# Hybrid pool/SSD block on one core: output projection's rows scaled, split and stored during the x, B, C columns, read back as finished 1 MB tiles

## The chip, the cores and the metric

The kernel runs on one core of a Trainium2 chip. The metric is the device time of one execution in microseconds (us); less is better. A profile comes from one profiled execution of its own.

## The reference, cut to what matters

```python
mod_lat = silu(c) @ w_ada + b_ada                  # g_l is its last third: the gate, one number per output column
hm   = rmsnorm(h) * (1 + scale) + shift            # 2048 latent and 256 context tokens, 1024 channels
p    = hm @ w_in                                   # pool input, pool gate, SSD gate, x/B/C (2048 columns), dt
xbc  = silu(depthwise_conv(p[..., x, B, C]))
y_s  = rmsnorm(bidirectional_scan(xbc, dt) * silu(z_ssd)) * ssd_norm_w
y_p  = pool_mixer(p[..., pool]) * pool_scale * silu(z_pool)
out  = rmsnorm(x + g_l * (concat([y_p, y_s]) @ w_out)) * final_norm_w
```

`pool_scale` and `ssd_norm_w` are one number per row of `w_out`, `g_l` is one per column. The kernel therefore multiplies them into `w_out` (2048 rows of 1024) once. It also splits each fp32 weight into a rounded part (hi) and the residual (lo), so that a product takes three matmuls: hi by hi, hi by lo, lo by hi.

## The kernel before, in words

Work runs in stages, each of them fed to TensorE as long rows of matmuls:

- **Start.** adaLN numbers, norms and modulated tokens `hm[0..3]` (each hi and lo) for 4 blocks of 512 tokens, and x/B/C columns 0 and 1.
- **The x, B, C columns**, `for ct in range(2, 16)` at L578 to L600: one tile of 128 columns of `w_in` at a time. `weights()` (L219) loads a raw 512 KB tile (`raw_weights`, L207), lets ScalarE round it to hi and GpSimd subtract for lo (`split_weights`, L212). TensorE then makes 24 matmuls over the context (columns below 12) and 24 for each of 4 token blocks. After each block ScalarE, VectorE and GpSimd do the convolution (L259), and `conv_store` (L246) writes the result to DRAM; for columns below 12 it is transposed and goes out through the SP queue in four DMAs a block. Column `ct` loads the weights of column `ct + 1` when it begins. Columns 5 to 8 also carry `late_pool_map` (L543), columns 10 to 13 two `gate_row` each (L563), which sum up the gate `gacc` from 512 KB loads.
- **The sweep** (upper token halves, L717 on): z, pool-gate and pool products, with the backward states between them. Here the gate is spread to all partitions (`gb`, two matmuls), and the lower 8 of the 16 row tiles of `w_out` are scaled (`rescale`, L723) and stored to `s_wo`.
- **The lower halves** (L760 on): the same products for the lower tokens, and box means on VectorE. `prepare(k)` (L856) loads a row tile of `w_out`, scales it if that is not done, and writes hi and lo into `wout0` or `wout1`.
- **The ramp** (`RAMP`, L1208): the first scan steps, an order written out by hand, with `prep_load`, `prep_scale`, `prep_hi`, `prep_lo` of tiles 5 to 8 among them; tiles 9 to 15 follow it. Then 64 steady steps of scan and output projection, by hand-written table too.

Outside the two hand-ordered parts a scheduler sets each engine's order from the program and its own estimate of time; on an engine or a DMA queue instructions then start in that order, and one that waits holds all behind it. Of the pools, `rawp` (`rpool`) has two 4 KB-per-partition buffers under the one tag `wraw`, taken in turn by every raw weight tile, gate row and row tile, and a new tile waits until the last reader of the tile two before it is done.

```python
rpool = rstack.enter_context(tc.tile_pool(name="rawp", bufs=2, side="right"))
wpool = wstack.enter_context(tc.tile_pool(name="wpool", bufs=2, side="right"))
```

Of the kernel before, what the change touches and what calls it, by code (L numbers as in the profile page):

```python
# [23 lines left out]
def hybrid_block(ctx, tc, d, out):  # L24
# [11 lines left out]
    def pp(name):  # L36
        return psum.tile([P, 512], F32, tag="pp", name=name)
# [24 lines left out]
    s_zp = dram("s_zp", [8, P, 1024])  # L62
    s_yp = dram("s_yp", [NCH, P, 8, P])
    s_af = dram("s_af", [P, 2, NC2, 16])
    s_gate = dram("s_gate", [P, 1024])
    s_wo = dram("s_wo", [8, P, 1024])
    s_rows = dram("s_rows", [2, NCH, 16, P])

    wstack = ExitStack()
# [256 lines left out]

    hc = dp.tile([P, 2, 8, 256], F32R, tag="hc", name="hc")
    dt_raw = const("dt_raw", [P, NC2, 32], pool=dp)
    wd = dp.tile([P, 8, P], F32R, tag="wd", name="wd")
    ctxt = Tokens(hc, 256, d["ctxT"], 1, "c", wpool.tile([P, 8, 256], F32, tag="w", name="xc"))  # L330
    ada = [slot(f"ada{a}", [P, 4, 2048], F32) for a in range(2)]
    cu = slot("cu", [P, 8192], F32)
# [230 lines left out]
    def gate_row(k):  # L563

        wg = rpool.tile([P, 1024], F32, tag="wraw", name=f"wg{k}")
        nc.sync.dma_start(wg, d["w_ada"][k * P:(k + 1) * P, 2048:3072])
        if k == 0:
            nc.vector.tensor_scalar(gacc, wg, scol[:, k, 0:1], None, op0=ALU.mult)
        else:
            nc.vector.scalar_tensor_tensor(gacc, wg, scol[:, k, 0:1], gacc, op0=ALU.mult, op1=ALU.add)  # L570
        if k == 7:
            brow = rpool.tile([1, 1024], F32, tag="wraw", name="brow")
            nc.sync.dma_start(brow, d["b_g"])
            nc.vector.tensor_tensor(gacc[0:1, :], gacc[0:1, :], brow, op=ALU.add)
# [5 lines left out]
    for ct in range(2, 16):  # L580
        next(tables, None)
        col = cols[ct]
        col.w = wx.pop(ct)
        if ct < 15:
            wx[ct + 1] = weights(d["w_xbc"][ct + 1], f"x{ct + 1}")
        if ct < 12:
            col.context()
            col.context_out()
        for b in range(4):
            col.block(b)  # L590
            col.block_out(b)
            col.conv()
            if ct > 12 and late:
                late.pop(0)()
        if 5 <= ct < 9:
            late_pool_map(2 + (ct - 5) // 2, (ct - 5) % 2)
        elif ct in (10, 11, 12, 13):
            for k in range(2):
                gate_row(2 * ct - 20 + k)
    gstack.close()  # L600
    cstack.close()
    dstack.close()
    tabs2 = ctx.enter_context(tc.tile_pool(name="tabs2", bufs=1))
    rowscale = const("rowscale", [P, 16], d["rowscale"], pool=tabs2)
    dskip = const("dskip", [P, 16], d["d_skip"].broadcast_to([P, 16]), pool=tabs2)
    allone = const("allone", [P, P], pool=tabs2)
    nc.vector.memset(allone, 1.0)
    mcol = const("mcol", [P, 1], pool=tabs2)
    nc.vector.memset(mcol, 1.0 / 256.0)
    hst = const("hst", [P, 4, 256], pool=tabs2)  # L610
# [102 lines left out]
    with tc.tile_pool(name="sweepp", bufs=2) as bp, tc.tile_pool(name="evp", bufs=3) as ep:  # L713
# [6 lines left out]
                count[0] -= 10  # L720
                next(sw, None)

        def rescale(raw, k):  # L723

            for j in range(2):
                js = raw[:, 512 * j:512 * j + 512]
                nc.vector.scalar_tensor_tensor(js, js, rowscale[:, k:k + 1], gb[j], op0=ALU.mult, op1=ALU.mult)

        upper = (2, 3)
        for j in range(8):  # L730
            w = weights(d["w_z"][j], f"z{j}_2")
            for b in upper:
                silus.append(z_block(ep, w, j, b, between if j else None))
                if j == 0 and b == 2:
                    next(sw)
            if j == 1:
                gacc = rpool.tile([P, 1024], F32, tag="wraw", name="gacc2")
                nc.sync.dma_start(gacc, s_gate)
                gb = [pp(f"gb{j}") for j in range(2)]
                for j in range(2):  # L740
                    mm(gb[j], allone, gacc[:, 512 * j:512 * j + 512], True, True)
            for k in {1: (), 7: (5, 6, 7)}.get(j, (j - 2,) if j else ()):
                raw = rpool.tile([P, 1024], F32, tag="wraw", name=f"wos{k}")
                nc.sync.dma_start(raw, d["w_out"][1024 + k * P:1152 + k * P, :])
                rescale(raw, 8 + k)
                nc.scalar.dma_start(s_wo[k], raw)
            for src, dst, fn in ((d["w_zp"][j], s_zp, AF.Silu), (s_wp[j], s_v, AF.Copy)):
                w = weights(src, f"p{j}_{fn}")
                for i, b in enumerate(upper):
                    t = ep.tile([P, 512], F32, tag="ev", name=f"e{j}_{b}_{fn}")  # L750
                    ps = pp(f"pp{j}_{b}_{fn}")
                    project(ps, w, hm[b], between)
                    nc.scalar.activation(t, ps, fn)
                    nc.scalar.dma_start(dst[j, :, 512 * i:512 * i + 512], t)
# [79 lines left out]
    bx = slot("bx", [P, 8192], F32)  # L834
    wout = [slot("wout0", [P, 4, 2, 1024], F32R)]

    raws = {}

    def prep_load(k):
        raws[k] = rpool.tile([P, 1024], F32, tag="wraw", name=f"wor{k}")  # L840
        nc.sync.dma_start(raws[k], s_wo[k - 8] if k >= 8 else d["w_out"][k * P:(k + 1) * P, :])

    def prep_scale(k):
        if k < 8:
            rescale(raws[k], k)

    def prep_hi(k):
        nc.scalar.copy(wout[k // 4][:, k % 4, 0, :], raws[k])

    def prep_lo(k, eng=None):  # L850
        wo = wout[k // 4][:, k % 4]
        eng = eng or (nc.gpsimd if k in (1,3,4,5,7,13,15) else nc.vector)
        eng.tensor_tensor(wo[:, 1, :], raws[k], wo[:, 0, :].bitcast(F32), op=ALU.subtract)  # L853

    def prepare(k):
        prep_load(k)  # L856
        prep_scale(k)
        prep_hi(k)
        prep_lo(k)

    with tc.tile_pool(name="boxp", bufs=1) as xp:
        for i, j in enumerate(order):
# [339 lines left out]
        wout.append(slot(f"wout{len(wout)}", [P, 4, 2, 1024], F32R))  # L1202

    kp = None
    other = {f.__name__: f for f in (prep_load, prep_scale, prep_hi, prep_lo, z, zg, logs, work, more)}

    RAMP = """
    0:load prep_load/5 1:load 0:scores 0:carried 0:shift 0:mask 0:exponents prep_scale/5 1:shift 0:steps_mix  # L1210
    prep_hi/5 logs 0:decay z/6/0 1:scores 1:carried zg/6/0 z/7/0 0:mix 0:from_states prep_load/6 
    0:mix2 1:mask 1:exponents 2:load prep_scale/6 1:steps_mix prep_hi/6 1:decay zg/7/0 2:scores 2:carried more
    1:from_states 1:mix 0:outputs z/6/1 prep_lo/5 prep_load/7 0:load_pool prep_lo/6
    0:gate 2:mask prep_scale/7 1:mix2 prep_load/8 1:load_pool 0:squares 2:shift
    2:steps_mix 0:square_sum 2:exponents 1:outputs 0:norm_mm z/7/1 more work prep_hi/8 prep_hi/7 zg/6/1 prep_lo/8
    0:state prep_lo/7 3:load 2:from_states 1:gate 0:pool_hi 1:squares zg/7/1 logs 0:norm1 
# [102 lines left out]
```

## Time and profile before

| | us |
|---|---|
| median of 3 runs (lowest, highest) | 1699.45 (1695.41, 1699.87) |
| the profiled execution's own time | 1695.88 |
| its span, first to last instruction | 1694.0 |
| busy in the span: TensorE (PE) | 1639.7 |
| VectorE (DVE) / ScalarE (ACT) / GpSimd (POOL) | 1222.8 / 766.9 / 596.5 |
| mean granted TensorE clock | 0.986 |

The busy time of PE is that of pipelined matmuls, whose ends are modelled. The stages can be told apart by the names that PE works on: `px` and `pc` are the x, B, C columns, `pz` and the pool products follow, `po` is the output projection. Times below count from the start of the span.

### The profile page before, as it was taken

To read this page: it belongs to the slowest core of one execution; us is meant where nothing else is said; L and a number is where in the kernel's file an instruction comes from. 1 tells how busy PE (TensorE), PEld (TensorE's weight loads), DVE (VectorE), ACT (ScalarE), POOL (GpSimd) and SP (SyncE) were. 2 spreads that over 40 slices of the span, in tenths; PEclk is the share of its full clock that TensorE was granted. 3 is DMA by queue.
4 is the path that set the end of the run, shared out by engine and by line. 5 is a ranking of instruction groups with operands and counts; after the bars stand their busy time and mean duration, and the time that the engine had idled before them with its cause. 6 is when DMAs were issued, how large, how long until landed. Compare 5 with 4: busy or idle time off the path is not lost. (4 is left out here: it accounts for less than half of the span.)

```text
span 1694.0 us, 25052 instructions
## 1 busy us (share of the span) xinstructions
PE 1639.7 (97%) x7798; PEld 1308.1 (77%) x7798; DVE 1222.8 (72%) x2516; ACT 766.9 (45%) x1857; POOL 596.5 (35%) x666
## 2 busy tenths in 40 slices
PE   8899999999998999999999989869999999999997
PEld 2788888888886788888887868757888888888886
DVE  1885655466685878776299998557788888888885
ACT  2763544434454444443212122455565556565663
POOL 1522111111124666665433334323333333333331
PEclk9999999999999999999999999989999999999999
DMA  9432344566554777778624355675667667666662
GB/s 375 177 118 69 77 101 96 135 166 149 155 126 144 241 252 235 247 246 275 212 84 151 113 186 185 187 225 172 193 194 208 194 198 206 193 210 191 197 192 83
DMA packets 313623, 303.11 MB, mean 179 GB/s; under 512 B 132753, under 2 KB 240145, under 8 KB 311186
## 3 DMA queue, kind: packets, MB, share of 16 engines
q1 hardware_dynamic: 239362, 233.60, 47.5%
q10 hardware_dynamic: 74128, 67.91, 12.0%
q8 instruction: 62, 1.02, 0.2%
q14 instruction: 71, 0.58, 0.1%
HBM read 207.81 MB, written 93.62 MB: 178 GB/s over the span
## 5 line engine op out<-in xcount | busy, mean ns | idle before, releaser
L52 PE MATMUL px<-hm,w_x 128*128 128x512 f32 x1536 | 365.6, 397 | 2.4 <-ACT hm L200 1.3
L52 PEld LDWEIGHTS px<-hm,w_x 128*128 128x128 f32 x1536 | 288.3, 188 | 71.9 <-DVE hm L203 1.5
L52 PE MATMUL po<-wout,yp 128*128 128x512 f32 x768 | 212.9, 413 | 0.0
L52 PE MATMUL po<-wout,ys 128*128 128x512 f32 x768 | 211.2, 411 | 0.0
L52 PE MATMUL pz<-hm,w_z 128*128 128x512 f32 x768 | 188.1, 398 | 1.1 <-POOL w_z L215 1.1
L265 DVE SCALAR_TENSOR_TENSOR cacc<-u,conv_w,cacc 128x512 f32<-128x512 f32 x168 | 135.5, 820 | 61.1 <-POOL u L315 42.1
L52 PEld LDWEIGHTS pz<-hm,w_z 128*128 128x128 f32 x768 | 144.8, 189 | 36.6 <-POOL w_z L215 1.5
L52 PEld LDWEIGHTS po<-wout,yp 128*128 128x128 f32 x768 | 135.9, 190 | 34.7 <-issue 10.6
L52 PEld LDWEIGHTS po<-wout,ys 128*128 128x128 f32 x768 | 136.3, 190 | 23.7
L962 POOL TENSOR_TENSOR yp<-yl,yp 128x256 fp32r<-128x256 f32 x64 | 50.2, 785 | 230.1 <-ACT yp L958 230.1
L647 DVE TENSOR_TENSOR xw<-xt,w_t 128x256 f32<-128x256 f32 x144 | 99.5, 729 | 19.8 <-POOL xr L654 12.4
L654 POOL TENSOR_TENSOR xr<-xw,xh 128x512 fp32r<-128x512 f32 x72 | 98.6, 1369 | 20.7 <-ACT xh L652 17.6
L962 POOL TENSOR_TENSOR ys<-yg,ys 128x256 fp32r<-128x256 f32 x64 | 62.7, 979 | 117.5 <-ACT ys L958 69.2
L652 ACT CAST xh<-xw 128x512 fp32r<-128x512 f32 x72 | 44.7, 621 | 119.5 <-PE st L52 72.6
L52 PE MATMUL pv<-hm,w_v 128*128 128x512 f32 x384 | 92.8, 401 | 5.9 <-ACT zt L797 5.9
L52 PE MATMUL ivationFunctionType.Silu<-hm,ivationFunctionType.Silu 128*128 128x512 f32 x384 | 96.7, 399 | 0.0
L52 PE MATMUL ivationFunctionType.Copy<-hm,ivationFunctionType.Copy 128*128 128x512 f32 x384 | 95.7, 395 | 0.0
L52 PE MATMUL pzp<-hm,w_q 128*128 128x512 f32 x384 | 91.3, 396 | 1.1 <-ACT va L790 1.1
L52 PEld LDWEIGHTS pv<-hm,w_v 128*128 128x128 f32 x384 | 73.5, 192 | 24.1 <-ACT zt L797 6.3
L937 DVE SCALAR_TENSOR_TENSOR m<-cbl,dt_t,m 128x128 f32<-128x128 f32 x256 | 84.2, 392 | 4.0 <-ACT m L929 4.0
L52 PEld LDWEIGHTS ivationFunctionType.Silu<-hm,ivationFunctionType.Silu 128*128 128x128 f32 x384 | 73.0, 190 | 18.1 <-issue 0.5
L52 PEld LDWEIGHTS pzp<-hm,w_q 128*128 128x128 f32 x384 | 72.0, 188 | 19.2 <-ACT va L790 1.6
(268 smaller groups left out, 3077.6 us busy)
## 6 DMA issues: line engine op xcount, KB each, us to landing
e<-s_rows SPq DMA_DIRECT2D x128, 256.0 KB, 4.9
s_tok<-tkw ACTq DMA_DIRECT2D x64, 256.0 KB, 3.1
bc<-s_bc SPq DMA_DIRECT2D x64, 256.0 KB, 4.2
st<-s_tok SPq DMA_DIRECT2D x64, 256.0 KB, 5.5
xt<-s_xt SPq DMA_DIRECT2D x72, 128.0 KB, 3.1
ada<-in_w_ada_dram SPq DMA_DIRECT2D x8, 1024.0 KB, 14.7
wraw_x<-in_w_xbc_dram SPq DMA_DIRECT2D x16, 512.0 KB, 4.2
s_bc<-cacc ACTq DMA_DIRECT2D x32, 256.0 KB, 3.1
```

Source lines behind the costliest of these rows:

```text
L52: nc.tensor.matmul(o, l, r, start=start, stop=stop)
L265: nc.vector.scalar_tensor_tensor(acc, u[:, k:k + n], conv_w[:, ct, k:k + 1], acc, op0=ALU.mult, op1=ALU.add)
L647: nc.vector.tensor_tensor(xw[:, s], h4(xt), w_t[:, s, c, 4 * g:4 * g + 4].unsqueeze(2).broadcast_to([P, 4, 64]), op=ALU.mult)
L652: nc.scalar.copy(xh, xw)
L654: nc.gpsimd.tensor_tensor(xr, xw, xh.bitcast(F32), op=ALU.subtract)
L937: nc.vector.scalar_tensor_tensor(s.m[:, h, :], s.cbl[:, 1, :], dt_t[:, 1, s.c, i:i + 1], s.m[:, h, :], op0=ALU.mult, op1=ALU.add)
L962: nc.gpsimd.tensor_tensor(y[:, 1], src, y[:, 0].bitcast(F32), op=ALU.subtract)
```

## The change

The finished row tiles now lie in DRAM as `s_wo[16, 128, 2, 1024]`, hi and lo for all 16. They are made in the columns' loop:

```diff
-    s_gate = dram("s_gate", [P, 1024])
-    s_wo = dram("s_wo", [8, P, 1024])
+    s_wo = dram("s_wo", [16, P, 2, 1024])
...
-            nc.scalar.dma_start(s_gate, gacc)
+            for j in range(2):
+                gb = aux(f"gb{j}")
+                mm(gb, allone, gacc[:, 512 * j:512 * j + 512], True, True)
+                nc.scalar.copy(gacc[:, 512 * j:512 * j + 512], gb)
+
+    def prep(k):
+
+        raw = rpool.tile([P, 1024], F32, tag="wraw", name=f"wos{k}")
+        nc.sync.dma_start(raw, d["w_out"][k * P:(k + 1) * P, :])
+        for j in range(2):
+            js = slice(512 * j, 512 * j + 512)
+            nc.vector.scalar_tensor_tensor(raw[:, js], raw[:, js], rowscale[:, k:k + 1], gacc[:, js],
+                                           op0=ALU.mult, op1=ALU.mult)
+            w = gp.tile([P, 2, 512], F32R, tag="wo", bufs=1, name=f"wo{k}_{j}")
+            nc.scalar.copy(w[:, 0], raw[:, js])
+            nc.gpsimd.tensor_tensor(w[:, 1], raw[:, js], w[:, 0].bitcast(F32), op=ALU.subtract)
+            nc.sync.dma_start(s_wo[k, :, :, js], w.bitcast(F32))
...
-        elif ct in (10, 11, 12, 13):
+        if 4 <= ct < 8:
             for k in range(2):
-                gate_row(2 * ct - 20 + k)
+                gate_row(2 * ct - 8 + k)
+        elif 8 <= ct < 12:
+            for k in range(4):
+                prep(4 * ct - 32 + k)
```

`rowscale` and the ones for `gb` move to the pool that opens before this loop. In the sweep `rescale`, the reload of the gate and the 8 loads and 8 stores of row tiles go. In the lower halves and the ramp each `prepare` is one DMA of 1 MB:

```diff
-    def prep_load(k):
...
     def prepare(k):
-        prep_load(k)
-        prep_scale(k)
-        prep_hi(k)
-        prep_lo(k)
+        nc.sync.dma_start(wout[k // 4][:, k % 4].bitcast(F32), s_wo[k])
```

The ramp's `prep_load/5` to `/8` become `prepare/5` to `/8` at the same places, and its `prep_scale`, `prep_hi` and `prep_lo` go. A small tile (`wd`) changes its pool.

How the order moves, at three places. First the SP queue, where column 10's raw weights (`wraw_x10`) are loaded; `u8_2` is block 2 of column 8 after its convolution, `uc9` the context part of column 9. Before:

```order
L253 DMA s_bt_67<-u8_0_2567 32x16x32 x4
L253 DMA s_bt_67<-u8_1_2607 32x16x32 x4
L209 DMA wraw_x10_2746<-in_w_xbc_dram 128x1024
L253 DMA s_bt_67<-u8_2_2648 32x16x32 x4
L253 DMA s_bt_67<-u8_3_2689 32x16x32 x4
L209 DMA wraw_x11_2956<-in_w_xbc_dram 128x1024
```

Now (`wos2` is the raw row tile 2, `wo2_1` its second half, split):

```order
L593 DMA s_wo_76<-wo1_1_2802 256x1x512
L585 DMA wos3_2818<-in_w_out_dram 128x1024
L252 DMA s_bt_67<-u9_1_2929 32x16x32 x4
L593 DMA s_wo_76<-wo2_0_2809 256x1x512
L252 DMA s_bt_67<-u9_2_2970 32x16x32 x4
L252 DMA s_bt_67<-u9_3_3011 32x16x32 x3
L593 DMA s_wo_76<-wo2_1_2814 256x1x512
L208 DMA wraw_x10_2830<-in_w_xbc_dram 128x1024
L252 DMA s_bt_67<-u9_3_3011 32x16x32
L593 DMA s_wo_76<-wo3_0_2821 256x1x512
```

The load of column 10's weights stood within column 8's stores. Now it stands behind three of the four stores of column 9's last block and behind the six half tiles `wo0_0` to `wo2_1`.

The same queue at column 13's weights, now:

```order
L593 DMA s_wo_76<-wo13_1_3576 256x1x512
L585 DMA wos15_3592<-in_w_out_dram 128x1024
L593 DMA s_wo_76<-wo14_0_3583 256x1x512
L593 DMA s_wo_76<-wo14_1_3588 256x1x512
L208 DMA wraw_x13_3604<-in_w_xbc_dram 128x1024
L593 DMA s_wo_76<-wo15_0_3595 256x1x512
L208 DMA wraw_x14_3753<-in_w_xbc_dram 128x1024
L593 DMA s_wo_76<-wo15_1_3600 256x1x512
```

Thirty of the 32 half tiles are stored before column 13's weights are asked for.

PE at column 10; `pc10` is the context's product, `px10_0` to `px10_3` the token blocks'. Before:

```order
L52 MATMUL pc10_2961<-hc_111,w_x10_2748 128x256 x24
L52 MATMUL px10_0_2990<-hm0_118,w_x10_2748 128x512 x24
L52 MATMUL px10_1_3030<-hm1_693,w_x10_2748 128x512 x24
L52 MATMUL px10_2_3071<-hm2_863,w_x10_2748 128x512 x24
L52 MATMUL px10_3_3112<-hm3_977,w_x10_2748 128x512 x24
```

Now:

```order
L52 MATMUL pc10_3093<-hc_110,w_x10_2832 128x256 x2
L52 MATMUL px10_0_3122<-hm0_117,w_x10_2832 128x512 x2
L52 MATMUL px10_1_3162<-hm1_692,w_x10_2832 128x512 x2
L52 MATMUL px10_2_3203<-hm2_862,w_x10_2832 128x512 x2
L52 MATMUL pc10_3093<-hc_110,w_x10_2832 128x256 x22
L52 MATMUL px10_0_3122<-hm0_117,w_x10_2832 128x512 x22
```

The first two matmuls of four groups, which need only the rounded weights, are drawn ahead of the rest, which needs the residual too; columns 11, 12 and 13 read alike.

## Rows read from the trace of the kernel before

**Rows 1.** Windows by stage: length; busy PE, PEld, DVE, ACT, POOL; granted clock; DMA share; GB/s.

```profile
332.00:497.00 165.00, 165.00 (x744) 134.56 (x743) 113.01 (x151) 73.58 (x116) 29.84 (x72) 1.00 0.65 155
...
525.00:832.00 307.00, 307.00 (x1313) 246.82 (x1312) 217.74 (x362) 125.67 (x278) 196.86 (x163) 1.00 0.74 238
...
1082.00:1160.00 78.00, 57.60 (x266) 44.47 (x265) 49.79 (x120) 45.34 (x99) 24.52 (x22) 0.85 0.66 203
```

**Rows 2.** Waits of PE: total us, times, longest.

```profile
PE yo L52 <- DMA st<-s_tok: 7.1, 1, 7.1
...
PE pv L52 <- ACT zt L797: 5.9, 1, 5.9
PE n L52 <- DVE dec_t L998: 3.6, 1, 3.6
```

**Rows 3.** Timeline of PE, columns 9 to 15: start, us, then the instruction.

```profile
328.51 3.62 PE L52 MATMUL pw<-wl,uT 128*128 128x256 f32 x16
...
357.23 3.04 PE L52 MATMUL pc<-hc,w_x 128*128 128x256 f32 x24
...
382.49 3.04 PE L52 MATMUL pc<-hc,w_x 128*128 128x256 f32 x24
385.37 112.15 PE L52 MATMUL px<-hm,w_x 128*128 128x512 f32 x480
```

**Rows 4.** Timeline of the SP queue around column 10's start.

```profile
352.56 0.35 SPq L209 DMA_DIRECT2D wraw_x<-in_w_xbc_dram  x1
...
365.87 3.20 SPq L253 DMA_DIRECT2D s_bt<-u  x4
```

**Rows 5.** Groups by form: busy us, mean ns | idle before.

```profile
L654 POOL TENSOR_TENSOR xr<-xw,xh 128x512 fp32r<-128x512 f32 x72 | 98.6, 1369 | 20.7 <-ACT xh L652 17.6 <-PE st L52 3.0
...
L652 ACT CAST xh<-xw 128x512 fp32r<-128x512 f32 x72 | 44.7, 621 | 119.5 <-PE st L52 72.6 <-DVE xw L647 28.9 <-DVE hb L683 4.6
...
L727 DVE SCALAR_TENSOR_TENSOR wos<-wos,rowscale,gb 128x512 f32<-128x512 f32 x16 | 11.3, 745 | 11.6 <-DMA wos<-in_w_out_dram 11.5
```

**Rows 6.** DMA issues: count, KB each, median us to landing.

```profile
wraw_x<-in_w_xbc_dram SPq DMA_DIRECT2D x16, 512.0 KB, 4.2
...
wos<-in_w_out_dram SPq DMA_DIRECT2D x8, 512.0 KB, 4.2
s_wo<-wos ACTq DMA_DIRECT2D x8, 512.0 KB, 3.1
...
s_gate<-gacc ACTq DMA_DIRECT2D x1, 512.0 KB, 5.3
```

**Rows 7.** DMA issues within 328:345, then within 355:372.

```profile
s_bc<-cacc ACTq DMA_DIRECT2D x2, 256.0 KB, 4.4
...
s_bc<-cacc ACTq DMA_DIRECT2D x3, 256.0 KB, 3.4
```

**Rows 8.** The tile s_wo: its transfers.

```profile
DMA to landing us min/median/max: 2.6/3.6/6.9
```

**Rows 9.** Timelines of ACT and POOL: column 11's weights split.

```profile
357.91 1.05 ACT L214 CAST w_x<-wraw_x 128x1024 fp32r<-128x1024 f32 x1
...
359.04 2.40 POOL L215 TENSOR_TENSOR w_x<-wraw_x,w_x 128x1024 fp32r<-128x1024 f32 x1 [0.78 <-ACT w_x L214]
```

**Rows 10.** Timeline of PE in the lower halves.

```profile
990.78 13.28 PE L52 MATMUL pv<-hm,w_v 128*128 128x512 f32 x48 [5.90 <-ACT zt L797]
...
1015.11 11.36 PE L52 MATMUL pv<-hm,w_v 128*128 128x512 f32 x48
```

**Rows 11.** Timeline of DVE in the lower halves and the ramp.

```profile
973.43 1.40 DVE L727 SCALAR_TENSOR_TENSOR wor<-wor,rowscale,gb 128x512 f32<-128x512 f32 x2
...
976.95 1.22 DVE L853 TENSOR_TENSOR wout<-wor,wout 128x1024 fp32r<-128x1024 f32 x1
...
1089.69 6.11 DVE L937 SCALAR_TENSOR_TENSOR m<-cbl,dt_t,m 128x128 f32<-128x128 f32 x4 [4.04 <-ACT m L929]
...
1100.29 1.13 DVE L937 SCALAR_TENSOR_TENSOR m<-cbl,dt_t,m 128x128 f32<-128x128 f32 x4
```

More of the change, by code (lines that the diff above doesn't have):

```diff
@@ L328, in hybrid_block @@
     dt_raw = const("dt_raw", [P, NC2, 32], pool=dp)
-    wd = dp.tile([P, 8, P], F32R, tag="wd", name="wd")
+    wd = sp.tile([P, 8, P], F32R, tag="wd", bufs=1, name="wd")
     ctxt = Tokens(hc, 256, d["ctxT"], 1, "c", wpool.tile([P, 8, 256], F32, tag="w", name="xc"))
@@ L488, in hybrid_block @@
     triL = const("triL", [P, P], d["triL"], pool=tabs)
+    rowscale = const("rowscale", [P, 16], d["rowscale"], pool=tabs)
+    allone = const("allone", [P, P], pool=tabs)
+    nc.vector.memset(allone, 1.0)
     n4 = [P, 2, NC2, 16]
@@ L603, in hybrid_block @@
     tabs2 = ctx.enter_context(tc.tile_pool(name="tabs2", bufs=1))
-    rowscale = const("rowscale", [P, 16], d["rowscale"], pool=tabs2)
     dskip = const("dskip", [P, 16], d["d_skip"].broadcast_to([P, 16]), pool=tabs2)
-    allone = const("allone", [P, P], pool=tabs2)
-    nc.vector.memset(allone, 1.0)
     mcol = const("mcol", [P, 1], pool=tabs2)
@@ L721, in between @@
                 next(sw, None)
[L723 to L727, printed above, removed]
         upper = (2, 3)
@@ L735, in hybrid_block @@
                     next(sw)
[L736 to L746, printed above, removed]
             for src, dst, fn in ((d["w_zp"][j], s_zp, AF.Silu), (s_wp[j], s_v, AF.Copy)):
@@ L835, in hybrid_block @@
     wout = [slot("wout0", [P, 4, 2, 1024], F32R)]
-    raws = {}
-    def prep_load(k):
[L840 to L853, printed above, removed]
     def prepare(k):
-        prep_load(k)
-        prep_scale(k)
-        prep_hi(k)
-        prep_lo(k)
+        nc.sync.dma_start(wout[k // 4][:, k % 4].bitcast(F32), s_wo[k])
     with tc.tile_pool(name="boxp", bufs=1) as xp:
@@ L1204, in hybrid_block @@
     kp = None
-    other = {f.__name__: f for f in (prep_load, prep_scale, prep_hi, prep_lo, z, zg, logs, work, more)}
+    other = {f.__name__: f for f in (prepare, z, zg, logs, work, more)}
     RAMP = """
[L1210 to L1216, printed above, removed]
+    0:load prepare/5 1:load 0:scores 0:carried 0:shift 0:mask 0:exponents 1:shift 0:steps_mix
+    logs 0:decay z/6/0 1:scores 1:carried zg/6/0 z/7/0 0:mix 0:from_states prepare/6
+    0:mix2 1:mask 1:exponents 2:load 1:steps_mix 1:decay zg/7/0 2:scores 2:carried more
+    1:from_states 1:mix 0:outputs z/6/1 prepare/7 0:load_pool
+    0:gate 2:mask 1:mix2 prepare/8 1:load_pool 0:squares 2:shift
+    2:steps_mix 0:square_sum 2:exponents 1:outputs 0:norm_mm z/7/1 more work zg/6/1
+    0:state 3:load 2:from_states 1:gate 0:pool_hi 1:squares zg/7/1 logs 0:norm1
     1:square_sum 0:norm2/0 1:pool_hi 2:decay 2:mix 0:pool_lo 1:pool_lo 3:scores 1:norm_mm 0:out/0/0
```

## The prediction

> **What bounds the kernel now.** I read the windows first. Across the x, B, C columns PE is busy for all 165.00 of 165 us, across the sweep for 307.00 of 307, both at full clock [rows 1]; the ramp is the one loose stage, 57.60 of 78 at a granted clock of 0.85. PE sets the time. An edit that only takes work off other engines in the first two stages gains nothing, and one that makes PE wait there costs what it makes it wait. The list of PE's waits [rows 2] says where something can be gained: 7.1 us for a load `st` in the ramp, 5.9 in the lower halves, 3.6 for `dec_t` in the ramp, and no wait in the columns. PE's timeline gives the columns' pace: column 10 begins at 357.23 and column 11 at 382.49, so 25.26 us for a column with context; 480 matmuls in 112.15 us make 22.4 for one without (column 12 on) [rows 3]. Last, the SP queue: before, the next column's weights are asked for at 352.56, and the four stores of column 9's last block are issued from 365.87 on, 0.8 each, 8.64 us after that block's last matmul (PE turned to column 10 at 357.23) [rows 3, 4].
>
> **What the columns now carry.** Sixteen row tiles, two halves each, are split through one tile, `wo`, with one buffer. A half's chain is: ScalarE's cast, GpSimd's subtract, the store, and only when the store has landed may the next cast write the buffer. Nothing of it can overlap with its successor, and eight halves fall to a column. The cast of the same shape takes 0.62 us, the subtract 1.37 [rows 5]. The handoffs: GpSimd's subtract began 0.08 after the cast's end (357.91 + 1.05 to 359.04) [rows 9]; three of these make 0.25.
>
> The store's landing is the unknown: no row shows a 512 KB store on SP in this stage. Nearest from below: the row tiles' own stores of 512 KB in the sweep, 3.1. From above: the gate's store, also 512 KB, in this stage, 5.3 [rows 6]. The 256 KB `s_bc` stores near column 10 took 4.4 and 3.4 [rows 7]; the smallest landing of any transfer of `s_wo` is 2.6 [rows 8]. I take 3.8, nearest to the two `s_bc` rows since they are of this stage, where the DMA share is 0.65 [rows 1]. A half then takes 0.62 + 1.37 + 3.8 + 0.25 = 6.04 us, and eight 48.3, where a column has 25.3.
>
> Two things join it. Raw tiles share two buffers with the weights: the first raw tile of a column reuses the buffer of the tile whose last half has just been subtracted, so its load (4.2 [rows 6], issue 0.4, scale 0.74 [rows 5]) stands where a landing of 3.8 stood: +1.6 a column. And one group of four `s_bt` issues, 3.2 [rows 4], falls between a store and its turn; the rest lie within landings. A column's chain is 48.3 + 1.6 + 3.2 = 53.1.
>
> This becomes PE's wait through SP. The order puts column 10's weights behind `wo2_1`, column 11's behind `wo6_1`, column 12's behind `wo10_1`, column 13's behind `wo14_1`; the buffer also frees only then. PE has eight matmuls to draw ahead, and those need the weights too.
>
> - Column 10: the first half is stored after column 8's last block: 328.51 (its last matmul [rows 3]) + 8.64 + 3.2 + 0.7 for two issues = 341.0. Five halves more, 30.2, and half an `s_bt` group, 1.6: the load is issued at 372.8, lands 4.2 later, is cast in 1.05 [rows 9] and starts PE at 378.4 with the handoffs. It was 357.2: **21.2**.
> - Columns 11 and 12: the chain's 53.1 less PE's 25.3, 27.8 each: **55.7**.
> - Column 13: column 12 has no `s_bt` stores, so 53.1 − 3.2 = 49.9, less 22.4: **27.5**.
> - Columns 14 and 15 wait for nothing more: their loads stand behind the two last halves, while column 13 runs.
>
> Together 104.4. After a wait PE restarts at a lower granted clock: 48 matmuls took 13.28 after the wait of 5.90, and 11.36 otherwise [rows 10]. Within the columns this hides under the chain; after the last wait it is paid: +1.9.
>
> **Elsewhere.** In the lower halves DVE no longer scales and subtracts ahead of the `zt` that ends the 5.9 wait: 1.40 + 1.22 [rows 11], −2.6. In the ramp `dec_t` sits right behind a row tile's subtract, a wait of 3.6 that should go [rows 2]; four `m` took 6.11 beside GpSimd's subtract where 1.13 is usual [rows 11], a stretch of 5.0 of which I count half, 2.5, as on the path. For the doubled bytes I give back 1: −5 in all. Bounds: all 20.4 idle us and 8 of slow clock gone (about −29); or the loads late (+13.6, the last rival).
>
> At nothing: the sweep's loads, scales and stores that go (PE has no gap there); the gate rows' move to columns 4 to 7 (one gate load in two buffers, with some 8 us to spare before the next weights; without it their price would show as a wait at columns 6 to 8); the two `gb` matmuls, which move from one full stage to another; the small tile's pool; the four 1 MB loads at the start of the lower halves, covered by PE's work on weights already split there.
>
> Sum: 104.4 + 1.9 − 2.6 − 5 = +98.7 on a span of 1694.0, 1792.7; the profiled execution took 1695.9, 1.9 more than its span, which gives **1795**. The median of the runs is 3.6 above that execution. A measurement of this kernel can tell about 0.3% from no change.
>
> **The rivals.**
>
> *Stores land as in the sweep.* Twenty-nine landings lie on the path (5 + 8 + 8 + 8). At 3.1 the time is 29 × 0.7 = 20 less: 1774. For it: same bytes, same target. Against: a busier mix of small packets in the columns, and 3.4 to 4.4 for half the bytes there [rows 7]. At 2.6, the least seen, 1760. The Trainium skill (DMA: Bandwidth & Descriptors, Anatomy of one DMA — SWDGE (gpsimd) path) gives about 2.0 us plus bytes at 436 GB/s, most of the constant being the receipt of the write, longest to HBM; it speaks against a store on a chain, and by it, as an estimate, a store of 0.5 MB lands in 3.2 and the time is 1777. The trace agrees for the sweep (3.1) and not for the gate's store (5.3).
>
> *Stores land as the gate's did.* At 5.3: 29 × 1.5 = 43.5 more, 1838. For it: the one 512 KB store in this stage. Against: it is one transfer.
>
> *The weights are not held (the other side).* If each half took no more than 25.26 / 8 = 3.16 us, landings of 0.9, and the last block's stores did not stand ahead of the load, no column would wait and only the gains remained: 1695.9 − 7.6 = 1688. It decides at SP: column 10's load must be issued by 350.9 (357.2 less 4.2, 1.05 and handoffs). Against: 2.6 is the least landing, and three stores of block 3 of column 9, whose matmuls end only at 357.2, stand ahead in the order. Even with free stores the order costs 8.64 + 2.4 + 0.4 + 4.2 + 1.05 + 0.3 = 17.0 at column 10, about 16.2 at column 11 (two stores ahead), 10.6 at column 12 (behind block 2 only): some 44, or 1734. That is the floor.
>
> *The ramp's loads collide.* `wout3`'s four 1 MB loads stand on SP ahead of the `e` and `st` of the first steps, where `st` already costs 7.1 [rows 2]. 4.19 MB at 308 GB/s (203 at a share of 0.66 [rows 1], an estimate) are 13.6 us; paid in full in place of the −5, 1795 + 18.6 = 1814.
>
> **How the numbers follow.** Chances: forecast 0.64, fast stores 0.18, slow stores 0.12, weights not held 0.02, ramp 0.04. The range 1750 to 1842 takes in the first three and the ramp, with a few us beyond 1760 and 1838 for the `s_bt` issues that I placed. Only the rival of the other side is faster, 0.03 with what I may have missed; 0.02 for no change; slower 0.95.
>
> **What would show it.** Right: four waits of PE at the starts of columns 10 to 13, of about 21, 28, 28 and 27 us, ended by the weights' cast or subtract; ScalarE's casts of `wo` waiting for the store of `s_wo`; a granted clock under 1 there; a landing near 3.8; the sweep still full; PE's idle grown from 54 to about 150 us. The 5.9 and 3.6 waits smaller or gone. Wrong: no wait at column 10, or waits below 15 us (the chain overlaps where I have it in series), waits of 35 (the landing is the gate's), or a longer `st` wait in the ramp.

## The result and the profile after

The changed kernel takes 1764.45 us (median of 4 runs, 1760.79 to 1765.50), the kernel before 1699.66 (4 runs): a ratio of 1.0381, 95% interval [1.0363, 1.0399], 65 us slower. The forecast was 1795, its range 1750 to 1842. The profiled execution took 1764.88 with a span of 1763.1.

Where the stages begin shows where the time went (first matmul of each by name):

| stage | before | after | change |
|---|---|---|---|
| start and x, B, C columns (to the first `pz`) | 497.4 | 583.0 | +85.6 |
| sweep (first `pz` to first `pv`) | 340.2 | 337.4 | −2.8 |
| lower halves (first `pv` to first `yo<-st`) | 245.4 | 237.4 | −8.0 |
| ramp and steady steps (to the span's end) | 611.0 | 605.3 | −5.7 |

The columns lose 85.6 us, and the other stages give 16.5 of them back. PE's waits of the changed kernel, to be held against [rows 2]:

```profile
PE pc L52 <- ACT w_x L213: 38.2, 2, 20.8
PE px L52 <- ACT w_x L213: 36.2, 2, 18.6
PE yo L52 <- DMA st<-s_tok: 11.0, 2, 6.8
...
PE st L52 <- ACT xh L670: 4.6, 1, 4.6
```

Four waits for the weights' cast, 74.4 us, are new; `pv <- zt` (5.9) and `n <- dec_t` (3.6) are gone. Two waits that neither [rows 2] nor the prediction names became shorter: the first `st` of the sweep waited 7.1 us for ScalarE's `xh` and now waits 4.6, and `n` in the ramp waited 7.9 in two for `dg` and now waits 4.1. The waits stand at the starts of columns 10, 11, 12 and 13 in PE's timeline, where [rows 3] had none:

```profile
379.80 0.80 PE L52 MATMUL pc<-hc,w_x 128*128 128x256 f32 x2 [20.79 <-ACT w_x L213]
...
424.96 0.79 PE L52 MATMUL pc<-hc,w_x 128*128 128x256 f32 x2 [17.42 <-ACT w_x L213]
...
470.93 25.37 PE L52 MATMUL px<-hm,w_x 128*128 128x512 f32 x96 [18.58 <-ACT w_x L213]
513.98 69.22 PE L52 MATMUL px<-hm,w_x 128*128 128x512 f32 x288 [17.67 <-ACT w_x L213]
583.03 11.36 PE L52 MATMUL pz<-hm,w_z 128*128 128x512 f32 x48
```

After its wait, column 12's 96 matmuls take 25.37 where 22.55 is usual; the clock granted from 470.9 to 496.4 is 0.88, against 1.00 from 333 to 357. The SP queue shows why the weights are late. These are the loads of columns 10 to 13:

```profile
373.48 0.61 SPq L208 DMA_DIRECT2D wraw_x<-in_w_xbc_dram  x1
...
419.08 0.61 SPq L208 DMA_DIRECT2D wraw_x<-in_w_xbc_dram  x1
...
463.92 0.68 SPq L208 DMA_DIRECT2D wraw_x<-in_w_xbc_dram  x1
...
508.42 0.54 SPq L208 DMA_DIRECT2D wraw_x<-in_w_xbc_dram  x1
```

They are 45.6, 44.8 and 44.5 us apart: eight halves of the row tiles. What a half costs stands in three views: the groups by form, the waits of ACT, and the DMA issues from 330 to 520.

```profile
L592 POOL TENSOR_TENSOR wo<-wos,wo 128x512 fp32r<-128x512 f32 x32 | 41.3, 1292 | 104.7 <-ACT wo L591 94.1 <-DMA s_bt<-u 5.6 <-DMA wraw_x<-in_w_xbc_dram 5.0
L588 DVE SCALAR_TENSOR_TENSOR wos<-wos,rowscale,gacc 128x512 f32<-128x512 f32 x32 | 24.1, 792 | 72.5 <-DMA wos<-in_w_out_dram 72.5
L591 ACT CAST wo<-wos 128x512 fp32r<-128x512 f32 x32 | 19.8, 618 | 76.2 <-DMA s_wo<-wo 74.4 <-DVE wos L588 1.7
```

```profile
ACT wo L591 <- DMA s_wo<-wo: 74.4, 27, 6.5
```

```profile
s_wo<-wo SPq DMA_DIRECT2D x32, 512.0 KB, 3.2
wos<-in_w_out_dram SPq DMA_DIRECT2D x16, 512.0 KB, 4.8
s_bc<-cacc ACTq DMA_DIRECT2D x18, 256.0 KB, 2.7
```

ScalarE stood 27 times before a cast until the store had landed (its total, 74.4, is the same number as that of PE's waits by chance). Cast 0.62, subtract 1.29, landing 3.2 and 0.25 of handoffs make 5.36, eight of them 42.9; the measured 44.5 to 45.6 leave 1.6 to 2.7 for the raw tile's load and the `s_bt` issues.

### The profile page after: what moved, and what is told of

It is laid out like the page before. It is cut to its first block, busy times and chain, and to the rows that moved or that the text cites. A ratio compares the mean times of both kernels' runs of the same rounds, so it can differ in the third digit from the quotient of the medians.

```text
span 1763.1 us, 25140 instructions
## 1 busy us (share of the span) xinstructions
PE 1648.7 (94%) x7798; PEld 1315.0 (75%) x7798; DVE 1196.3 (68%) x2507; ACT 772.6 (44%) x1875; POOL 627.1 (36%) x691
## 4 chain that ended last, share of the span: by engine, by line
PE 55%; DVE 7%; DMA 6%; ACT 2%; issue 1%; POOL 1%; SPq 0%; ACTq 0%; DVEq 0%; POOLq 0%
PE po L52 21%; PE pz L52 6%; PE ivationFunctionType.Copy L52 5%; PE ivationFunctionType.Silu L52 5%; PE pv L52 4%; PE yo L52 3%; PE st L52 3%; PE pzp L52 3%; PE y L955 2%; PE y L961 2%; DVE bx L824 2%; DVE bx L814 2%; PE n L52 1%; DVE cacc L264 1%; DMA s_bc<-z 1%
## 5 line engine op out<-in xcount | busy, mean ns | idle before, releaser
L52 PE MATMUL px<-hm,w_x 128*128 128x512 f32 x1536 | 374.9, 403 | 38.2 <-ACT w_x L213 36.2
L52 PEld LDWEIGHTS px<-hm,w_x 128*128 128x128 f32 x1536 | 293.6, 192 | 110.5 <-ACT w_x L213 37.1
L264 DVE SCALAR_TENSOR_TENSOR cacc<-u,conv_w,cacc 128x512 f32<-128x512 f32 x168 | 131.3, 797 | 64.8 <-POOL u L314 44.8
L665 DVE TENSOR_TENSOR xw<-xt,w_t 128x256 f32<-128x256 f32 x144 | 90.4, 666 | 15.4 <-POOL xr L672 15.4
L886 ACT ACTIVATE e<-e,nrb_t 128x128 f32<-128x128 f32 x256 | 81.1, 387 | 11.7 <-DMA tk<-s_xt 7.7
```

Source lines behind the costliest of these rows:

```text
L52: nc.tensor.matmul(o, l, r, start=start, stop=stop)
L264: nc.vector.scalar_tensor_tensor(acc, u[:, k:k + n], conv_w[:, ct, k:k + 1], acc, op0=ALU.mult, op1=ALU.add)
L665: nc.vector.tensor_tensor(xw[:, s], h4(xt), w_t[:, s, c, 4 * g:4 * g + 4].unsqueeze(2).broadcast_to([P, 4, 64]), op=ALU.mult)
L886: nc.scalar.activation(s.e2[:, h, :], s.e2[:, h, :], AF.Identity, bias=nrb_t[:, s.c, 4 * s.g + h:4 * s.g + h + 1])
```

## The experiments

Two questions were open. Is it the serial chain that holds the weights, or something else that came with it (the queue they stand in, the DMA engines)? And why did the lower halves gain 8.0 where 2.6 was counted?

**What holds the weights.** The first run takes the landing out of the series: quarters instead of halves, with two buffers in the same memory.

```diff
-        for j in range(2):
-            js = slice(512 * j, 512 * j + 512)
+        for j in range(4):
+            js = slice(256 * j, 256 * j + 256)
...
-            w = gp.tile([P, 2, 512], F32R, tag="wo", bufs=1, name=f"wo{k}_{j}")
+            w = gp.tile([P, 2, 256], F32R, tag="wo", bufs=2, name=f"wo{k}_{j}")
```

> Row tiles split in quarters of 256 columns with two buffers of 2 KB instead of halves with one of 4 KB; same memory, same bytes, 64 stores of 256 KB. Theory (the store's landing stands in series because wo has one buffer): a landing now overlaps the other quarter's cast and subtract. A quarter then costs (0.37 cast + 0.75 subtract + 2.7 landing, as the 256 KB s_bc stores of the changed kernel took, + 0.25) / 2 = 2.0 us, sixteen 32.6, a column's chain about 34 instead of 45; the four waits of PE shrink from 84 us in all (restarts included) to about 40, time about 1720. Rival A (the SP queue's order alone holds the weights, the landing does not matter): twice as many stores stand ahead of the weights, no gain, 1760 or more. Rival B (the DMA engines' throughput bounds the chain): same bytes, 1764.

Measured: 1750.22 us, 1.0309 [1.0288, 1.0329]. The waits are 18.0, 13.4, 16.4 and 12.5, 60.3 in all instead of 74.4, and the columns start 41 to 44 us apart, later 37. That is a part of the gain that the theory gave (1720 was expected), so this run alone decides little: it excludes only that nothing would change. The landing did not leave the series: with two buffers ScalarE's casts still waited 46 times, 65.6 us in all, for a store of `s_wo`. The 256 KB stores, two in flight, landed in 2.9 us where 2.7 was counted for one:

```profile
s_wo<-wo SPq DMA_DIRECT2D x64, 256.0 KB, 2.9
```

The second run moves the stores to GpSimd's queue, so that on SP nothing that waits for a split stands ahead of the weights.

```diff
-            nc.sync.dma_start(s_wo[k, :, :, js], w.bitcast(F32))
+            nc.gpsimd.dma_start(s_wo[k, :, :, js], w.bitcast(F32))
```

> The stores of the split halves are issued on GpSimd's queue instead of SP's, all else the same; wo keeps one buffer and the raw tiles still share their two buffers with the weights. Theory (the chain cast, subtract, landing in series, passed on to the weights by the shared raw buffers): the cycle from column to column stays at 45 us if the landing stays near 3.2, the four waits remain, 1750 to 1775. Rival A (the weights are late because they stand behind stores on SP): nothing that waits for a split stands ahead of them on SP any more, so the waits go, about 1690.

Measured: 1804.36 us, 1.0626 [1.0611, 1.0642], 40 us slower than the change. PE's waits, SP's own waits within 330 to 640, and the stores within 330 to 510:

```profile
PE px L52 <- ACT w_x L213: 58.6, 2, 30.5
PE pc L52 <- ACT w_x L213: 54.0, 2, 30.9
```

```profile
SPq L208 <- POOL wo L592: 37.8, 4, 12.5
```

```profile
s_wo<-wo POOLq DMA_DIRECT2D x24, 512.0 KB, 4.7
```

The rival (the stores in SP's queue) falls: free of them, SP does not bring the weights sooner. The second view names the link: four times SP stood before a load of weights (L208) until GpSimd's subtract of `wo`, the last reader of a row tile, was done. And the size fits the theory. From this queue a store lands in 4.7 instead of 3.2; the prediction's 29 landings on the path make 29 × 1.5 = 43.5, the run lost 40. The condition "if the landing stays near 3.2" was not met, which is why the time is outside the 1750 to 1775 that stood there.

The third run divides the two raw buffers while the columns run: one for the weights, one for row tiles, gate rows and the pool map's small tile. Same memory, same four tiles per column.

```diff
-    rpool = rstack.enter_context(tc.tile_pool(name="rawp", bufs=2, side="right"))
+    rpool = rstack.enter_context(tc.tile_pool(name="rawp", bufs=1, side="right"))
...
-        raw = rpool.tile([P, 1024], F32, tag="wraw", name=f"wos{k}")
+        raw = rpool.tile([P, 1024], F32, tag=rtag(True), name=f"wos{k}")
```

(`rtag` gives `ra` for weights and `rb` for the others within the loop, and both in turn elsewhere.)

> The changed kernel with its two raw buffers divided while the columns run: one for the weights alone, one for gate rows, row tiles and the pool map's small tile; same memory, same four row tiles per column, wo still one buffer, stores still on SP. Theory (the chain of cast, subtract and landing is slow, and reaches PE through the shared raw buffers, which put each column's weights behind the last row tiles): the waits at columns 10 to 13 go to under 3 us each although the chain is no faster; with one raw buffer a tile takes 2 x 5.45 - 3.2 + 5.3 = 13.0 us, sixteen end near 341 + 208 = 550, and the sweep's first loads, behind the last store on SP, come some 30 to 50 us late: 1715 to 1740. Rival A (the weights are late because SP, ScalarE and GpSimd stand in their order behind splits and stores, whoever owns the raw buffer): waits of 10 us and more stay at columns 10 to 13, 1765 or more.

Measured: 1757.63 us, 1.0363 [1.0346, 1.0381]. The time is above the 1715 to 1740 expected. The waits for the columns' weights are gone; PE's timeline runs through columns 10 to 14, and PE's largest wait now stands at the sweep's start:

```profile
384.10 3.04 PE L52 MATMUL pc<-hc,w_x 128*128 128x256 f32 x24
...
419.63 68.51 PE L52 MATMUL px<-hm,w_x 128*128 128x512 f32 x292
491.42 5.86 PE L52 MATMUL px<-hm,w_x 128*128 128x512 f32 x24 [3.28 <-ACT u L316]
```

```profile
PE ivationFunctionType.Silu L52 <- ACT ivationFunctionType.Silu L220: 76.3, 1, 76.3
```

So the chain reached PE through the shared raw buffers: with a chain that is no faster, no column waits for weights any more. The run changes the order on SP too (column 10's weights are now asked for at 342.95, ahead of every store); that the stores' place on SP is not the cause, the run before shows. The first `pz` comes at 504.4, near the 497.4 of before. The price at the sweep was 76, not the 30 to 50 expected. ScalarE's timeline and SP's show the two reasons:

```profile
543.28 0.62 ACT L598 CAST wo<-wos 128x512 fp32r<-128x512 f32 x1 [6.76 <-DVE wos L595]
548.31 0.62 ACT L598 CAST wo<-wos 128x512 fp32r<-128x512 f32 x1 [4.41 <-DMA s_wo<-wo]
556.35 0.62 ACT L598 CAST wo<-wos 128x512 fp32r<-128x512 f32 x1 [7.42 <-DVE wos L595]
...
587.57 0.62 ACT L598 CAST wo<-wos 128x512 fp32r<-128x512 f32 x1 [4.42 <-DMA s_wo<-wo]
594.88 1.04 ACT L220 CAST ivationFunctionType.Silu<-ivationFunctionType.Silu 128x1024 fp32r<-128x1024 f32 x1 [6.70 <-DMA ivationFunctionType.Silu<-in_w_zp_dram]
```

```profile
584.51 5.55 SPq L600 DMA_DIRECT2D s_wo<-wo  x2
590.16 0.55 SPq L215 DMA_DIRECT2D ivationFunctionType.Silu<-in_w_zp_dram  x1
```

With nothing else to do a tile takes 13.07 us (543.28 to 556.35), as worked out, but beside the convolutions it took more, so the sixteenth ended near 588 and not 550; and the load of the sweep's `Silu` weights is issued only behind the last store. The DMA engines do not bound the chain: they were busy for 0.33 of that last stretch (543.3 to 588), where a tile still took its 13.07.

**How much of the chain fits.** Five runs place the tiles elsewhere; one of them divides the raw buffers as well. The first gives four columns' work to eight:

```diff
-        elif 8 <= ct < 12:
-            for k in range(4):
-                prep(4 * ct - 32 + k)
+        elif ct >= 8:
+            for k in range(2):
+                prep(2 * ct - 16 + k)
```

> Two row tiles per column in columns 8 to 15 instead of four in columns 8 to 11. Theory: four halves are 4 x 5.45 = 21.8 us, under a column's 25.3 and 22.4, so the waits at columns 10 to 13 go to below 3 us each; but the chain of 32 halves from 341 on ends near 341 + 174 + 10 = 525, and the sweep's first weights, which stand behind the last tiles in the shared raw buffers, come some 20 to 26 us late: 1694 - 15 (what the later stages gained) + 2 + 20 to 26, about 1705. Rival A (the order on SP holds each column's weights by 10 to 17 us whatever the number of tiles): six or seven columns wait, 1740 or more.

Measured: 1724.13 us, 1.0149 [1.0131, 1.0168]. The large waits of columns 10 to 13 are gone (8.7 us in three waits for a cast remain), and 27.7 us for the first `w_z` stand at the sweep's start. Rival A falls; the expectation, 1705, was some 19 us too low. The small waits in the columns come to 13.5 us where 2 stood, and PE restarts slowly after each.

In the next, gate rows stand in columns 2 to 5 and tiles in 6 to 14:

```diff
...
+        if 2 <= ct < 6:
+            for k in range(2):
+                gate_row(2 * ct - 4 + k)
+        elif ct in (6, 7):
+            prep(ct - 6)
+        elif 8 <= ct < 15:
+            for k in range(2):
+                prep(2 * ct - 14 + k)
...
```

> Gate rows in columns 2 to 5, one row tile each in columns 6 and 7, two each in columns 8 to 14. Theory: four halves fit in a column (21.8 us against 25.3 and 22.4) and the last split is done before the sweep, so at most a few us of waiting are left in the columns and only the gains of the later stages remain (the changed kernel took 14.9 us less than the kernel before from the sweep's first matmul on): 1681 to 1692, faster than the kernel before. Rival A (the order on SP holds the weights whatever the number of tiles): 1740 or more. Rival C (the gains of the later stages came only from the work having been done during PE's waits, and go with them): 1697 to 1703.

Measured: 1708.38 us, 1.0064 [1.0046, 1.0082]; the 1681 to 1692 expected was missed. From the first `pz` on it takes 1182.8 where the kernel before takes 1196.6: the later stages keep their gain without PE's long waits, so rival C falls. But the columns end 25 us later than before: with two tiles a column PE still waits at columns 12 and later, 0.8 to 4.0 us at a time, and 100 matmuls take 26.37 after one:

```profile
416.32 1.22 PE L52 MATMUL px<-hm,w_x 128*128 128x512 f32 x2 [4.01 <-ACT w_x L213]
419.12 26.37 PE L52 MATMUL px<-hm,w_x 128*128 128x512 f32 x100 [1.57 <-POOL u L317]
```

The next run has divided raw buffers, gate rows in columns 2 and 3, and tiles in columns 4 to 14 by two or one:

```diff
...
+        for k in {2: [0, 1, 2, 3], 3: [4, 5, 6, 7]}.get(ct, ()):
+            gate_row(k)
+        for k in {4: [0, 1], 5: [2], 6: [3, 4], 7: [5], 8: [6, 7], 9: [8], 10: [9, 10], 11: [11], 12: [12, 13], 13: [14], 14: [15]}.get(ct, ()):
+            prep(k)
...
```

> Divided raw buffers as in sep, and the work spread out: gate rows in columns 2 and 3, row tiles in columns 4 to 14 by two or one (2, 1, 2, 1, 2, 1, 2, 1, 2, 1, 1). Theory: a tile takes 13 us, two 26, in columns of 28.7 and 25.3, one in those of 22.4, so nothing waits in the columns and the chain is done before the sweep; the gains of the later stages stay (13 to 15 us from the sweep's first matmul on, gb's move apart 11 to 13): 1682 to 1692, faster than the kernel before by 0.4 to 1%. Rival A (each order on SP, ScalarE and GpSimd that mixes splits into the columns costs some us per column): 1695 to 1710, as the kernel with tiles in columns 6 to 14, which waited in eight places.

Measured: 1711.57 us, 1.0095 [1.0079, 1.0110]. The 1682 to 1692 expected was missed; rival A's range, 1695 to 1710, is nearest. No wait for the columns' weights is in the list, but new ones stand there: 7.7 us of `px` for ScalarE's copy of `u` and 7.1 of a `pw` for its activation of `cacc`. ScalarE's casts of `wo` waited 13 times, 33.6 us, for a scaled row tile and 12 times, 15.9, for a store, and the evacuations stand behind them in its order. That this alone made PE wait is not shown: right before the two longest waits for `u` (4.3 and 2.3) ScalarE stood for a store of `cacc` (3.5) and for a reload `ur` (5.7).

The next has shared buffers again, with two tiles in each of columns 4 to 9, among them those with the pool map (5 to 8), and one each in 10 to 13:

> Shared raw buffers as in the change; gate rows in columns 2 and 3, two row tiles each in columns 4 to 9, one each in columns 10 to 13. Theory: four halves with their share of loads take 24 to 25 us, less than columns 4 to 9 last (28.7, column 9 25.3), two halves 12 in the later ones, so no column waits more than 2 us: 1683 to 1694, faster than or level with the kernel before. Rival A (the weights' load behind the preceding stores on SP costs 4 us and more in every column whatever its number of tiles): 1700 or more.

Measured: 1721.46 us, 1.0154 [1.0139, 1.0169]. The 1683 to 1694 expected was missed, and the same chain comes out in a third place:

```profile
PE pw L52 <- DMA uT<-in_w_uT_dram: 16.9, 3, 6.1
```

The pool map's `uT` shares the raw buffers too. Columns 11 to 15, with one tile each or none, ran without a gap (480 matmuls in 112.16). From both comes the last placing, one tile beside the pool map and two in most other columns:

```diff
...
+        for k in {2: [0, 1, 2], 3: [3, 4, 5], 4: [6, 7]}.get(ct, ()):
+            gate_row(k)
+        for k in {4: [0], 5: [1], 6: [2], 7: [3], 8: [4, 5], 9: [6, 7], 10: [8, 9], 11: [10, 11], 12: [12, 13], 13: [14], 14: [15]}.get(ct, ()):
+            prep(k)
```

> Shared raw buffers as in the change; gate rows 3, 3, 2 in columns 2 to 4, row tiles 1 each in columns 4 to 7, 2 each in columns 8 to 12, 1 each in 13 and 14. Theory (a column waits where its share of the chain, 12 us per tile, does not fit in it, and hardly elsewhere; with two tiles beside the pool map two kernels ago it waited 5 to 6 us a column, with one it did not; two in a 22.4 us column cost 2 to 5): about 6 us of waits and restarts left in the columns, the later stages 13 to 15 us shorter than before: 1684 to 1694, 0.2 to 0.7% faster than the kernel before. Rival (each order that mixes splits into the columns costs 15 to 30 us there, wherever the tiles stand, because ScalarE, in whose queue the split of a half waits for a landing, then also evacuates TensorE's results late): 1700 to 1712.

Measured: 1703.04 us, 1.0038 [1.0024, 1.0052], the best of the five and still slower than the kernel before. Columns 5 to 8 run without a wait; 10 us remain at columns 12 and 13 and 6.3 for the sweep's `Silu` weights. The 1684 to 1694 expected was missed, and the rival's range, 1700 to 1712, holds it. No placing that was tried pays. The rival's reason, evacuations that come late on ScalarE, is argued and not shown; what this run shows is that most of what remains in the columns is still waits for the weights' cast (7.4 of the 10).

**Why the lower halves gained 8.0.** After the first trace the reason seemed to be VectorE's order: before, the next box's first sum (4.69) stood ahead of the `zt` that PE waits for. So the dead work was put back, and the order with it:

```diff
                 prepare(i - 4)
+                r = rpool.tile([P, 1024], F32, tag="wraw", name=f"back{k}")
+                nc.sync.dma_start(r, d["w_out"][k * P:(k + 1) * P, :])
+                for j in range(2):
...
+                    nc.vector.scalar_tensor_tensor(r[:, js], r[:, js], rowscale[:, k:k + 1], r[:, js],
+                                                   op0=ALU.mult, op1=ALU.mult)
+                nc.vector.tensor_tensor(r, r, r, op=ALU.subtract)
```

> The changed kernel with dead work put back into the lower halves: beside each of the four 1 MB loads a row tile of w_out is loaded into a raw buffer, scaled by VectorE in two halves and subtracted from itself once (0.70 + 0.70 + 1.2 us as before), used by nobody. VectorE's order then again has the next box's first sum ahead of the zt of the box before. Theory (the stage gained 8.0 us, not 2.6, because with the scales gone zt also moved ahead of that sum of 4.7 us, and the restart after the wait went): the wait of about 6 us for zt comes back with its restart, 6 to 9 us more than the changed kernel: 1770 to 1774. Rival (only the 2.6 us of scales and subtract counted; the rest of the 8 was won elsewhere, by fewer loads or by ScalarE): 2 to 3 us more, 1767.

Measured: 1766.55 us, 1.0414 [1.0397, 1.0430]. The theory that VectorE's order alone made the wait fell: from the first `pv` to the ramp's first `yo` (`yo<-hst`) it takes 237.4 us where the change takes 237.0, and PE does not wait although `zt` is late. ScalarE can evacuate the product `pzp` only at 1070.25, when the earlier `zt` has been stored, yet PE has begun the next product at 1067.09:

```profile
1067.09 11.36 PE L52 MATMUL pv<-hm,w_v 128*128 128x512 f32 x48
```

```profile
1070.25 1.09 ACT L798 ACTIVATE zt<-pzp 128x512 f32<-128x512 f32 x2 [1.86 <-DMA s_yp<-zt]
```

Before, PE stood still until just that activation, and went on at 990.78 [rows 10]:

```profile
990.14 1.09 ACT L797 ACTIVATE zt<-pzp 128x512 f32<-128x512 f32 x2 [3.55 <-DMA s_yp<-zt]
```

So PE had a PSUM buffer free that it lacked before. The code says which: `gb`, the spread gate, was two of the four buffers of the products (`pp`) and stayed there from the sweep until the ramp's last scale. The change copies it back to `gacc` and frees both; the diff says so in one line that the prediction passed over. Three runs set this against VectorE's work. The first is the kernel before, with the gate moved to the other group of PSUM buffers (`aux`), idle in that stage, and copied back ahead of the ramp:

```diff
+    g2 = [aux(f"ga{a}") for a in range(2)]
+    for a in range(2):
+        nc.scalar.copy(g2[a], gb[a])
+    gb[:] = g2
     estack = ExitStack()
...
```

> The kernel before with one difference: the two PSUM tiles that hold the spread gate (taken from the four buffers of the products) are copied at the start of the lower halves into two buffers of the other PSUM group, idle in that stage, and copied back ahead of the ramp. Loads, scales, VectorE's order: as before. Theory B (the stage gained mainly because the change no longer holds two of the products' four PSUM buffers there): the wait of 5.9 us for ScalarE's zt goes with its restart of 1.9; the stage from the first pv to the ramp's first yo falls from 245.4 us to 238 to 241, the kernel to about 1690, 0.2 to 0.4% faster than before. Rival (the scales and subtracts on VectorE made that wait): nothing changes, 1696.

Measured: 1692.99 us (median of 12 runs), 0.9984 [0.9972, 0.9996]. The wait of 5.9 is gone, with every scale still in place: PE goes on at 983.49 although the activation comes at 988.88.

```profile
983.49 11.36 PE L52 MATMUL pv<-hm,w_v 128*128 128x512 f32 x48
```

```profile
988.88 1.09 ACT L801 ACTIVATE zt<-pzp 128x512 f32<-128x512 f32 x2 [4.06 <-DMA s_yp<-zt]
```

The stage gains 3.6 us by this and not the whole; PE, now earlier, meets two new waits for GpSimd's split of the weights:

```profile
PE pv L52 <- POOL w_v L215: 2.6, 2, 1.8
```

The other two are the changed kernel with two buffers held, and with both the buffers and the dead work put back:

```diff
             if j == 1:
+                held = [pp(f"held{a}") for a in range(2)]
+                for h in held:
+                    nc.vector.memset(h, 0.0)
...
+        for h in held:
+            nc.vector.tensor_tensor(bx[:, 0:512], bx[:, 0:512], h, op=ALU.mult)
```

> The changed kernel with two of the products' four PSUM buffers held from the sweep's second column to the end of the lower halves (cleared once, read once at the end), as the spread gate held them before; no other work. Theory B: the sweep loses 1 to 3 us, the lower halves (237.4 us) little, since zt of the fifth box is stored at 1066.4, before TensorE needs its PSUM buffer at 1067.6: 0 to 3 us. In all 1765 to 1770. Rival: as the changed kernel, 1764.

Measured: 1763.80 us, 1.0395 [1.0376, 1.0414], level with the change, as the rival said (1765 to 1770 was expected): alone the held buffers cost the stage nothing. So VectorE's order does matter. Before, the next box's first sum stood ahead of the `zt` that PE waits for:

```profile
978.09 4.69 DVE L813 TENSOR_TENSOR bx<-va 128x2240 f32<-128x2240 f32 x1
982.70 2.28 DVE L830 TENSOR_TENSOR zt<-bx,zt 128x2048 f32<-128x2048 f32 x1
```

In the changed kernel, with two buffers held, `zt` comes first, 2.4 us after the product's start at 1052.66 instead of 9.2 (973.53 before), and PE goes on with no wait:

```profile
1055.04 2.30 DVE L835 TENSOR_TENSOR zt<-bx,zt 128x2048 f32<-128x2048 f32 x1
1057.25 4.69 DVE L818 TENSOR_TENSOR bx<-va 128x2240 f32<-128x2240 f32 x1
```

```profile
1063.86 11.37 PE L52 MATMUL pv<-hm,w_v 128*128 128x512 f32 x48
```

> The changed kernel with both put back: the two held PSUM buffers and the dead scales and subtracts on VectorE. Theory B: with the scales alone zt's store landed at 1070.25, 3.2 us after TensorE could have begun the next product; with two PSUM buffers fewer it must wait for it: a wait of 3 to 6 us with a restart of about 2, the lower halves at 243 to 247 us, near the 245.4 of before, where either alone gives 237 to 241. Rival (scales alone): 240, as with them alone.

Measured: 1771.10 us, 1.0435 [1.0418, 1.0452], and the wait is back, with the slow restart behind it; `zt` starts 7.0 us after the product (1059.05 against 1052.10).

```profile
1067.62 13.64 PE L52 MATMUL pv<-hm,w_v 128*128 128x512 f32 x48 [4.16 <-ACT zt L802]
```

The table gives the stage from the first `pv` to the first `yo<-hst`, in us. (Up to the first `yo<-st`, as in the table of the stages, the ramp's wait for a load `st` counts in, 1.2 to 2.3 us in the three runs that put something back; before and in the change there is none at that place.)

| | buffers free | two buffers held |
|---|---|---|
| no scales on VectorE | 237.0 (the change) | 237.0 |
| scales on VectorE | 237.4; 241.3 (before, gate in `aux`) | 243.6; 244.9 (before) |

In the changed kernel either alone costs 0.0 or 0.4, together 6.6: the wait needs both the held buffers and the late `zt`, and the change took both away. The Trainium skill (Perfetto Trace Analysis, Identifying Performance Opportunities) says that repeated gaps on the engine that should be saturated can mean too little SBUF or PSUM for the next tile. The trace agrees in part: this was one gap of 5.9 us and not a repeated one, freeing two buffers closed it, and so did the earlier `zt` with the buffers held.

## Why the prediction was right, and where its sizes were off

- **The mechanism** (one `wo` buffer puts landings in series, shared raw buffers pass the chain to the weights): right. Shown by the 27 waits of ScalarE, by SP's four waits for `wo` in the run with stores on GpSimd's queue, by the run with divided buffers (waits gone) and by the size of the loss with slower stores (29 landings at 1.5 more: 43.5 worked out, 40 measured).
- **Column 10**, 21.2: measured 20.8, PE at 379.80 where 378.4 stood (1.6 of it are the `gb` matmuls that now lie ahead). Part of this is luck: the first half was stored at 343.8 and not 341.0, and the five halves after it took 29.1 and not 31.8, so the load was issued at 373.5 where 372.8 stood.
- **Columns 11 to 13**, 27.8, 27.8, 27.5: the step that was oversized. The waits are 17.4, 18.6 and 17.7; a column's cycle is 44.5 to 45.6, not 53.1 (49.9 for the last). Of the 8 us by which the first two are off, about 5 are the landing (3.2, not 3.8: 8 × 0.6) and 0.6 the subtract (1.29, not 1.37); the rest is the group of `s_bt` issues and the load, counted at 4.8 and worth 1.6 to 2.7. Choosing 3.8 by the stage's smaller stores was wrong; the row with the same bytes and target, 3.1 in the sweep, was the better one. The rival with that landing, 1774, came nearest. The Trainium skill (DMA: Bandwidth & Descriptors, Anatomy of one DMA — SWDGE (gpsimd) path) gives its fit for DMAs issued by GpSimd; by it, as an estimate, a store of this size lands in 3.2. The trace agrees for SP's queue, the median there being 3.2, and not for GpSimd's, where it was 4.7.
- **Restarts** at a lower clock: as said, hidden under the chain, but for the last. Columns 13 to 15 take 69.05 instead of three times 22.43: 1.8, where 1.9 stood. The clock granted from 513.9 to 520 is 0.67, from 520 to 583 it is 1.00.
- **Lower halves**, −2.6: wrong, −8.0. The 2.6 us of scales and subtract were taken off the wait one for one. The runs show that the whole wait of 5.9 and the restart of 1.9 behind it go when `zt` moves ahead of the next box's first sum, as it did with the scales gone, and that freeing the two PSUM buffers would have closed the wait too. The prediction saw neither: `gb`'s move was counted for its matmuls alone.
- **Ramp**, −5: measured −5.7 from there to the end. The `dec_t` wait (3.6) went, and the waits for `dg`, which the sum does not name, fell from 7.9 to 4.1, while those for `st` grew from 7.1 to 11.0; so the size is right, and its make-up in part luck. The colliding loads did not come to pass.
- **At nothing**: held in the columns. Columns 4 to 8 run as before but for `gb`, 1.6 us (column 9's context at 333.40 instead of 331.77), and no wait stands at the lower halves' first loads. The sweep is 2.8 us shorter, where nothing stood. That PE has no gap there was read from a window that begins at 525, and the sweep's one wait, 7.1 us for `xh`, ends at 524.23; it fell to 4.6, which is 2.5 of the 2.8. Why is not shown.

In the rival of the other side the latest issue of column 10's load comes out at about 351.6 from the terms named there, not 350.9; nothing else rests on it.

In sum +98.7 was forecast and +69.1 came on the span: 106.3 for the columns were 85.6 with `gb`, 7.6 of gains were 16.5.

## What to carry to other kernels

Before work goes into a stage that PE fills, find its longest serial chain (here cast, subtract, store, landing through one buffer) and ask which pool it shares with what PE needs next. Dividing that pool took the waits out of the columns, but the chain was as long as ever and came out as one wait of 76 us at the sweep, so both the link and the length have to be dealt with. When a change frees or pins PSUM or SBUF tiles, count the buffers left to each rotation in every stage they live through: here a wait stood only where two buffers were pinned and `zt` was late as well, and taking away either closed it. A DMA or GpSimd share that looks spare is not spare room in an in-order queue: in all five placings PE still waited in the columns for something that a queue brought late.

## What was not expected

The 512 KB store lands in 3.2 us from SP and 4.7 from GpSimd's queue, beside the same work. Held PSUM buffers and scales on VectorE cost the lower halves 0.0 and 0.4 us alone and 6.6 together. And the only version found that beats both kernels keeps the kernel before as it was and moves the two gate tiles to the idle group of PSUM buffers: 1692.99 us beside 1696.34 of the kernel before, measured with it, 0.9984 [0.9972, 0.9996], a gain of 0.16%. Whether the change's gains of 16.5 us after the columns can be had without its loss in them stays open; none of the five placings did it.
